# The mLSTM decay rows of a hybrid trunk are loaded through GpSimd's DMA queue instead of the sync engine's

## The chip, the cores and the metric

The kernel runs on one core of one Trainium2 chip. Its time is that of one execution on the device, in microseconds (us). The engines are named as in the profile: PE is TensorE's matmuls and PEld its weight loads, DVE is VectorE, ACT is ScalarE, POOL is GpSimd and SP is SyncE. A "q" behind an engine's name means its sequencer: SPq is the queue from which SyncE starts DMAs.

## What is computed

The reference is a decoder trunk of two layers over a sequence of 1024 positions with a width of 1024, in float32. In each layer one normalized input goes through one projection, and three groups of heads read it: an RG-LRU, a differential attention and an mLSTM. Their outputs are joined by one output projection; a causal conv-gated MLP follows. The change lies in the mLSTM, which the reference writes as a recurrence over chunks of 64 positions, for each of 4 heads of 128 features:

```python
D = jnp.where(causal, b[..., :, None] - b[..., None, :] + li[..., None, :], -jnp.inf)
m_t = jnp.maximum(m_inter, jnp.max(D, axis=-1))
w_intra = jnp.einsum('bhtd,bhsd->bhts', qc, kc) * jnp.exp(D - m_t[..., None])
inter = jnp.exp(m_inter - m_t)
num = inter[..., None] * jnp.einsum('bhtd,bhde->bhte', qc, C) + jnp.einsum('bhts,bhse->bhte', w_intra, vc)
den = inter * jnp.einsum('bhtd,bhd->bht', qc, n) + jnp.sum(w_intra, axis=-1)
h = num / jnp.maximum(jnp.abs(den), jnp.exp(-m_t))[..., None]
```

Every weight between a query t and a key s is the score q.k times the exponential of a decay. The kernel keeps that shape, with chunks of 512 positions instead of 64.

## The kernel before

`hybrid_trunk` runs, for each of the two layers, `mixer` (the heads and the output projection) and `ffn`. Nearly all matmuls keep float32 accuracy by splitting each operand into a high and a low part (`split`, lines 128 to 130: the high part is written by ScalarE, line 129, the low part by VectorE, line 130) and by three matmuls (`mm3`, lines 137 to 139).

The mixer is a list of steps, given by hand for each layer (`ORDER`, line 32). Steps "z" project the mLSTM's inputs, "A" are the attention, "R" the RG-LRU, "M" the mLSTM heads, "y" and "w" the output projection. A step only says in which order the program is written. The instructions of each engine are put in order when the program is built, by priority and estimated time, so that in the trace the steps interleave; evacuations and splits of weights are written with a raised priority (`high_priority(PRI)`). On the chip every engine and every DMA queue then works through its own list in that order: an instruction that waits holds up what stands behind it on the same engine. Tiles come from pools: a tag has so many buffers (`bufs`), and a new tile waits until a buffer of its tag has been used for the last time.

`ml_rows` (line 661) computes the decays of a layer: 32 rows of 1024 numbers, one for each of 8 blocks of 128 keys and 4 heads. It stores them to the DRAM tensor `Rd` (line 709), from which the heads read them back.

`ml_head(l, h, hf)` (line 780) does one head for one half of the positions, eight times in each layer (steps M0 to M7, two for each head). The queries and keys are loaded from DRAM and split; then four blocks of 128 keys follow (`jj`, line 806), each with n = 512, 384, 256 or 128 queries:

- one row of `Rd` is loaded into a tile R of 128 partitions, the same row in each (line 812). Its buffers have the tag "mr" with three buffers, which it shares with E and with `kt` (line 757);
- GpSimd masks the diagonal block (`affine_select`, line 813), ScalarE takes the exponential (line 814);
- TensorE computes the scores `ms` (line 816); VectorE multiplies them with R (line 817);
- the product is split into W (lines 129 and 130), and three matmuls add it, times the values, to the output `pn` (line 821);
- GpSimd adds R to the running sum `ds` (line 823 or 825), from which TensorE later forms the denominators (`tail`, line 832).

In the second half (`hf` = 1) the state of the first half comes in ahead of the blocks: one more row of `Rd` is loaded into E in the same way (line 798); ScalarE takes its exponential, VectorE multiplies it with the queries, and GpSimd starts `ds` from it (line 805). At the end of the first half `ml_state_out` (line 751) forms that state.

All loads and stores of the heads are issued from SyncE (`nc.sync.dma_start`), and so are the weight loads (`wblock`, line 113). GpSimd issues two kinds: `rgacc`, where each RG-LRU block adds its squares to a sum in DRAM (line 461; the first block stores, the other three accumulate), and, in the MLP, weight pieces that are added onto others (line 1120). `rg_sum` (line 467) reads the finished `rgacc` back through SyncE; the store of the RG-LRU's output itself (`yd`, line 459) goes through SyncE too.

Of the kernel before, what the change touches and what calls it, by code (L numbers as in the profile page):

```python
# [17 lines left out]
P = 128  # L18
# [3 lines left out]
HALF = 512  # L22
# [32 lines left out]
class Trunk:  # L55
# [724 lines left out]
    def ml_head(self, l, h, hf):  # L780
        nc, d = self.nc, self.lay[l]
        if hf == 0:
            self.ml_state[h] = [self.o4("num"), self.sm("mpc", (P, 16)), None]
        num, pc, state = self.ml_state[h]
        kscale = 0.25 * P ** -0.5
        qst = self.st_half(self.mqd[h][:, hf * HALF : (hf + 1) * HALF])
        qh, ql = self.qkt("qh"), self.qkt("ql")
        self.split(qst, qh, ql)
        kst = self.st_half(self.mkd[h][:, hf * HALF : (hf + 1) * HALF])
        kh, kl = self.qkt("kh"), self.qkt("kl")  # L790
        self.split(kst, kh, kl)
        vh, vl = self.vv(self.mvd, h, hf)
        pn = self.aux()
        ds = self.tp.tile([P, HALF], F32, tag="ds", bufs=1, name=self.nm("ds"))
        if hf:
            ch, cl, nv = state
            E = self.tp.tile([P, HALF], F32, tag="mr", bufs=3, name=self.nm("E"))
            nc.sync.dma_start(E, self.Rd[16 + h : 17 + h, HALF:].broadcast_to([P, HALF]))
            nc.scalar.activation(E, E, AF.Exp, bias=self.mle[:, 16 + h : 17 + h])
            nc.vector.tensor_tensor(E, E, qst, ALU.mult)  # L800
            W = self.p4("W", F32R)
            wh, wl = W[:, :HALF], W[:, HALF:]
            self.split(E, wh, wl)
            self.mm3(pn, [((ch, cl), (wh, wl))], stop=False)
            nc.gpsimd.tensor_scalar(ds, E, nv, None, ALU.mult)
        for jj in range(4):
            j = 4 * hf + jj
            n = HALF - jj * P
            js = slice(jj * P, jj * P + P)
            o = slice(jj * P, HALF)  # L810
            R = self.tp.tile([P, HALF], F32, tag="mr", bufs=3, name=self.nm("R"))
            nc.sync.dma_start(R[:, :n], self.Rd[4 * j + h : 4 * j + h + 1, j * P : (hf + 1) * HALF].broadcast_to([P, n]))
            nc.gpsimd.affine_select(R[:, :P], R[:, :P], [[1, P]], ALU.is_ge, -1e30, base=0, channel_multiplier=-1)
            nc.scalar.activation(R[:, :n], R[:, :n], AF.Exp, bias=self.mla[:, j, h : h + 1])
            sc = self.sc.tile([P, S], F32, tag="sc", name=self.nm("ms"))
            self.mm3(sc[:, :n], [((kh[:, js], kl[:, js]), (qh[:, o], ql[:, o]))])
            nc.vector.scalar_tensor_tensor(R[:, :n], sc[:, :n], kscale, R[:, :n], ALU.mult, ALU.mult)
            W = self.p4("W", F32R)
            wh, wl = W[:, :n], W[:, HALF : HALF + n]
            self.split(R[:, :n], wh, wl)  # L820
            self.mm3(pn[:, o], [((vh[:, js], vl[:, js]), (wh, wl))], start=j == 0, stop=jj == 3)
            if j == 0:
                nc.gpsimd.tensor_scalar(ds, R[:, :n], 1.0, 0.0, ALU.mult, ALU.add)
            else:
                nc.gpsimd.tensor_tensor(ds[:, o], ds[:, o], R[:, :n], ALU.add)
        if hf == 0:
            self.ml_state[h][2] = self.ml_state_out(h, kst, (vh, vl))
        nc.scalar.copy(num[:, hf * HALF : (hf + 1) * HALF], pn)
        def tail():
            pd = self.aux()  # L830
            for i in range(4):
                nc.tensor.matmul(pd[:, i : i + 1], ds[:, i * P : (i + 1) * P], self.ones_1, start=True, stop=True)
            nc.scalar.activation(pc[:, 8 + 4 * hf : 12 + 4 * hf], pd[:, 0:4], AF.Abs)
            if hf == 0:
                return
            sq = self.o4("sq")
            nc.scalar.activation(sq, num, AF.Square)
            pq = self.aux()
            self.compact(pq, sq, self.ones_h)
            f, v, r = self.sm("mf", (P, 8)), self.sm("nv", (P, 8)), self.sm("nr", (P, 8))  # L840
            nc.vector.tensor_tensor(f, pc[:, 8:16], self.mem[:, :, h], ALU.max)
            nc.vector.reciprocal(f, f)
            nc.vector.tensor_tensor(v, pq[:, 0:8], f, ALU.mult)
            nc.vector.tensor_tensor(v, v, f, ALU.mult)
            nc.vector.tensor_scalar(v, v, EPS, None, ALU.add)
            self.rsqrt(r, v)
            nc.vector.tensor_tensor(r, r, f, ALU.mult)
            th = self.p4("th")
            nc.sync.dma_start(th, self.mod[h])
            nc.vector.scalar_tensor_tensor(num, th, 1.0, num, ALU.add, ALU.mult)  # L850
            for j in range(2):
                t = slice(j * HALF, (j + 1) * HALF)
                nc.vector.scalar_tensor_tensor(num[:, t], num[:, t], d["mn2"][:, h : h + 1],
                                               self.bcast_half(r, j, self.ps), ALU.mult, ALU.mult)
            self.yd[8 + h] = self.dr("yd")
            nc.sync.dma_start(self.yd[8 + h], num)

        if h == 3 and hf:
            tail()
        else:  # L860
            self.tails.append(("M", tail))
# [479 lines left out]
```

## Time and profile before

| | |
|---|---|
| three runs | 2951.89, 2963.69 and 2966.23 us; median 2963.69 us |
| the profiled execution | 2952.44 us; its span 2950.7 us |
| mean granted clock of TensorE | 0.991 of full speed |
| busy share of the span | PE 97%, PEld 79%, DVE 70%, ACT 46%, POOL 8% |
| DMA | 353.58 MB, 120 GB/s on average |
| chain that ended last | PE 79%, DVE 8%, DMA 6%, ACT 3%, issue 3%, POOL 1% |

The profile is one execution, and its durations belong to it. The busy share of TensorE comes from matmuls that overlap, so 97% doesn't mean that it works at its peak; what counts is where it stands idle, for whom, and at which clock it then runs (1.00 in the column PEclk is full speed, 2.4 GHz; 0.50 is 1.2 GHz). A wait is put down to the work that ended it. The chain is followed from the last instruction back, at each step to what released it. "L812" is line 812 of the kernel; a line inside a helper, such as 129 or 137, stands for all that call it.

### The profile page before, as it was taken

Reading aid. Unit: us, or ns where it says so; the run is one execution under the profiler, and the core shown is the slowest. Engines: PE = TensorE matmul, PEld = TensorE weight load, DVE = VectorE, ACT = ScalarE, POOL = GpSimd, SP = SyncE. Lnnn points to the kernel's source line nnn. Section 1 sums busy time; section 2 is a strip of 40 time slices with the busy share of each in tenths; the row PEclk is TensorE's granted clock in tenths of the full one; section 3 lists DMA queues with packets and bytes.
Section 4 is the critical chain, followed back from the end, with each engine's and each line's share of the span. In section 5 each row is a group of like instructions: output and inputs, shape, how many; then the busy total and the mean of one; then the engine's idle time right before and its main releaser. Section 6 shows DMA issues by size and latency. Waiting matters only on the chain.

```text
span 2950.7 us, 36646 instructions
## 1 busy us (share of the span) xinstructions
PE 2863.7 (97%) x13262; PEld 2322.1 (79%) x13262; DVE 2055.0 (70%) x3369; ACT 1343.7 (46%) x2154; POOL 248.4 (8%) x312
## 2 busy tenths in 40 slices
PE   8999999989999999999999999998999999999998
PEld 6877777777788888788777877787877888887887
DVE  5775778776798888743484388787758888887334
ACT  4424656643554444421342256566426544444224
POOL 1000001111100000000000000202111000000000
PEclk9999999999999999999999999999999999999999
DMA  4332223463344454532423222325533544446223
GB/s 151 99 110 77 90 90 96 141 206 121 118 119 127 126 129 122 190 128 75 143 87 98 100 76 93 106 87 173 170 113 115 132 129 125 116 113 230 89 74 111
DMA packets 177029, 353.58 MB, mean 120 GB/s; under 512 B 20656, under 2 KB 47792, under 8 KB 176848
## 3 DMA queue, kind: packets, MB, share of 16 engines
q1 hardware_dynamic: 162144, 323.19, 34.1%
q0 software_dynamic: 13824, 27.27, 5.6%
q8 instruction: 104, 1.70, 0.2%
q10 hardware_dynamic: 880, 0.79, 0.1%
q14 instruction: 77, 0.63, 0.1%
HBM read 264.66 MB, written 86.51 MB: 119 GB/s over the span
## 4 chain that ended last, share of the span: by engine, by line
PE 79%; DVE 8%; DMA 6%; ACT 3%; issue 3%; POOL 1%; SPq 0%; DVEq 0%; POOLq 0%; ACTq 0%
PE z L138 23%; PE z L139 23%; PE z L137 23%; DMA R<-Rd 2%; DMA fst<-fa 1%; PE pbc L217 1%; PE aux L223 1%; DVE wlo L130 1%; PE sc L616 1%; PE aux L137 1%; PE aux L138 1%; PE sc L617 1%; PE aux L632 1%; PE aux L139 1%; DMA rgacc<-rg 1%
## 5 line engine op out<-in xcount | busy, mean ns | idle before, releaser
L129 ACT CAST whi<-wraw 128x512 fp32r<-128x512 f32 (+1 forms) x416 | 254.0, 612 | 689.5 <-PE z L138 516.4
L130 DVE TENSOR_TENSOR wlo<-wraw,whi 128x512 fp32r<-128x512 f32 (+1 forms) x416 | 284.7, 685 | 149.8 <-ACT whi L129 147.7
L138 PE MATMUL z<-hl,whi 128*128 128x512 f32 x896 | 360.5, 402 | 4.7 <-DVE hl L242 4.7
L137 PE MATMUL z<-hh,whi 128*128 128x512 f32 x896 | 361.3, 403 | 0.8 <-DVE mpad L416 0.8
L139 PE MATMUL z<-hh,wlo 128*128 128x512 f32 x896 | 360.4, 402 | 0.0
L137 PE MATMUL z<-ah,whi 128*128 128x512 f32 x704 | 272.8, 393 | 6.0 <-ACT ah L129 6.0
L137 PE MATMUL z<-xh,whi 128*128 128x512 f32 x704 | 274.6, 391 | 3.4 <-ACT cv L1151 3.4
L138 PE MATMUL z<-xh,whi 128*128 128x512 f32 x704 | 274.9, 390 | 1.9 <-DVE xh L130 1.9
L138 PE MATMUL z<-ah,whi 128*128 128x512 f32 x704 | 274.8, 392 | 0.6 <-DVE ah L130 0.4
L139 PE MATMUL z<-ah,wlo 128*128 128x512 f32 x704 | 274.6, 391 | 0.0
L139 PE MATMUL z<-xh,wlo 128*128 128x512 f32 x704 | 273.7, 389 | 0.0
L1128 DVE SCALAR_TENSOR_TENSOR fc<-cv,fpar,fc 128x1024 f32<-128x1024 f32 x176 | 221.7, 1279 | 5.9 <-ACT fc L1125 0.6
L129 ACT CAST whi<-fraw 128x512 fp32r<-128x512 f32 x180 | 111.5, 619 | 249.8 <-PE z L138 245.4
L137 PE MATMUL z<-xu,whi 128*128 128x512 f32 x528 | 209.3, 396 | 0.6 <-ACT cv L1151 0.6
L138 PE MATMUL z<-xu,whi 128*128 128x512 f32 x528 | 208.9, 396 | 0.0
L139 PE MATMUL z<-xu,wlo 128*128 128x512 f32 x528 | 208.8, 396 | 0.0
L138 PEld LDWEIGHTS z<-hl,whi 128*128 128x128 f32 x896 | 171.7, 192 | 40.6 <-DVE hl L242 9.0
L137 PEld LDWEIGHTS z<-hh,whi 128*128 128x128 f32 x896 | 171.8, 192 | 32.2 <-DVE mpad L416 0.9
L139 PEld LDWEIGHTS z<-hh,wlo 128*128 128x128 f32 x896 | 171.7, 192 | 31.4
L137 PEld LDWEIGHTS z<-ah,whi 128*128 128x128 f32 x704 | 131.9, 188 | 38.1 <-ACT ah L129 9.1
L137 PEld LDWEIGHTS z<-xh,whi 128*128 128x128 f32 x704 | 132.2, 188 | 32.0 <-ACT cv L1151 3.7
L1151 DVE TENSOR_TENSOR cv<-z,cv 128x512 f32<-128x512 f32 x132 | 90.9, 688 | 95.1 <-PE z L139 95.0
(374 smaller groups left out, 6026.3 us busy)
## 6 DMA issues: line engine op xcount, KB each, us to landing
wraw<-in_w_up_dram SPq DMA_DIRECT2D x128, 256.0 KB, 3.7
wraw<-in_w_in_dram SPq DMA_DIRECT2D x112, 256.0 KB, 2.8
wraw<-in_w_down_dram SPq DMA_DIRECT2D x112, 256.0 KB, 2.7
fraw<-in_w_up_dram SPq DMA_DIRECT2D x92, 256.0 KB, 2.9
fraw<-in_w_up_dram POOLq DMA_DIRECT2D x88, 256.0 KB, 5.0
fa<-fc SPq DMA_DIRECT2D x44, 512.0 KB, 3.9
fa<-fa SPq DMA_DIRECT2D x28, 512.0 KB, 5.3
wraw<-in_w_out_dram SPq DMA_DIRECT2D x48, 256.0 KB, 2.7
```

Of the source, the lines that this page charges most:

```text
L129: self.nc.scalar.copy(hi, src)
L130: self.nc.vector.tensor_tensor(lo, src, hi.bitcast(F32), ALU.subtract)
L137: nc.tensor.matmul(out, ah, bh, start=start and i == 0, stop=False, **kw)
L138: nc.tensor.matmul(out, ah, bl, start=False, stop=False, **kw)
L139: nc.tensor.matmul(out, al, bh, start=False, stop=stop and i == last, **kw)
L217: nc.tensor.matmul(pb[:, i * P : (i + 1) * P], r[:, c : c + 1].broadcast_to([P, P]), self.ident, start=True, stop=True)
L223: self.nc.tensor.matmul(pc[:, i : i + 1], sq[:, i * P : (i + 1) * P], ones, start=True, stop=True)
L616: nc.tensor.matmul(dst, qq[c][:, qs], k[:, :kn], start=True, stop=False)
L617: nc.tensor.matmul(dst, ql[c][:, qs], k[:, :kn], start=False, stop=kb < g)
L632: nc.tensor.transpose(pa[:, k * P : (k + 1) * P], pp[0][:, (4 * kb + k) * P : (4 * kb + k + 1) * P], self.ident)
L1128: nc.vector.scalar_tensor_tensor(o, u[:, j : j + S], cw[:, j, col : col + 1], o, ALU.mult, ALU.add)
L1151: fn(*x)
```

## The change

The two loads from `Rd` in `ml_head` are issued from GpSimd's queue instead of SyncE's. Their sources, destinations, sizes and buffers stay as they are: 4 loads of R in each of 8 steps in each of two layers, 64 in all, and 8 of E.

```diff
-            nc.sync.dma_start(E, self.Rd[16 + h : 17 + h, HALF:].broadcast_to([P, HALF]))
+            nc.gpsimd.dma_start(E, self.Rd[16 + h : 17 + h, HALF:].broadcast_to([P, HALF]))
...
-            nc.sync.dma_start(R[:, :n], self.Rd[4 * j + h : 4 * j + h + 1, j * P : (hf + 1) * HALF].broadcast_to([P, n]))
+            nc.gpsimd.dma_start(R[:, :n], self.Rd[4 * j + h : 4 * j + h + 1, j * P : (hf + 1) * HALF].broadcast_to([P, n]))
```

## Rows read from the trace of the kernel before

**Rows 1.** page, part 1: busy us (share of the span) xinstructions of each engine

```profile
PE 2863.7 (97%) x13262; PEld 2322.1 (79%) x13262; DVE 2055.0 (70%) x3369; ACT 1343.7 (46%) x2154; POOL 248.4 (8%) x312
```

**Rows 2.** mixers' stretches: us, each engine's busy us, PEclk, DMA share, GB/s

```profile
150.00:700.00 550.00, 526.31 (x2643) 426.94 (x2644) 400.89 (x731) 286.94 (x502) 60.52 (x83) 0.98 0.37 115
...
1560.00:2180.00 620.00, 596.75 (x2962) 482.44 (x2961) 427.85 (x795) 306.80 (x534) 67.62 (x87) 0.98 0.35 112
```

**Rows 3.** TensorE's waits, whole span: us in total, times, longest us

```profile
PE aux L137 <- ACT W L129: 8.9, 4, 6.0
PE aux L832 <- POOL ds L825: 7.8, 9, 2.3
...
PE aux L138 <- DVE W L130: 7.1, 8, 1.5
```

**Rows 4.** chain that ended last, heads: by line; pieces (start, us, what)

```profile
by line: PE z L139 9.1%; PE z L138 9.0%; PE z L137 8.7%; DMA R<-Rd 7.1%; issue 4.7%; PE aux L223 4.0%; PE pbc L217 3.2%; PE aux L138 2.6%; PE aux L139 2.4%; PE aux L137 2.4%; DVE wlo L130 2.4%; POOL ds L825 2.3%; PE aux L632 2.2%; DVE W L13
...
436.08 3.81 DMA E<-Rd
...
683.82 6.34 DMA R<-Rd
...
697.25 3.14 DMA R<-Rd
...
by line: DMA R<-Rd 10.8%; PE z L139 9.4%; PE z L138 9.2%; PE z L137 8.9%; issue 6.9%; PE aux L223 3.8%; POOL ds L825 2.7%; PE pbc L217 2.7%; DMA st<-vd 2.0%; DVE W L130 2.0%; PE aux L137 1.9%; DVE wlo L130 1.9%; PE aux L138 1.9%; DVE R L817
...
1855.55 2.77 DMA R<-Rd
...
2054.13 5.09 DMA R<-Rd
```

**Rows 5.** line 812's DMAs of R: ns min/median/max on the queue; us to landing

```profile
L812 SPq DMA_DIRECT2D R<-Rd x64: 319/320/895, 154.4 to 2150.3; - x64
...
DMA to landing us min/median/max: 2.8/4.2/6.9
```

**Rows 6.** the sync queue's own waits, whole span: us in total, times, longest us

```profile
SPq L113 <- DVE wlo L130: 724.2, 219, 16.3
...
SPq L812 <- DVE W L130: 70.1, 32, 8.0
...
SPq L467 <- DMA rgacc<-rg: 9.4, 2, 6.5
```

**Rows 7.** two lines on GpSimd: its DMAs, its sums: ns min/median/max

```profile
L1120 POOL DMA_DIRECT2D fraw<-in_w_up_dram x88: 842/863/1188, 735.6 to 2638.3; - x88
...
L825 POOL TENSOR_TENSOR ds<-ds,R x56: 455/1020/2600, 417.8 to 2155.6; 128x384 f32<-128x384 f32 x16, 128x256 f32<-128x256 f32 x16, 128x128 f32<-128x128 f32 x16, 128x512 f32<-128x512 f32 x8
```

**Rows 8.** 512 KB transfers to landing: line 461 (GpSimd); yd among the issues

```profile
DMA to landing us min/median/max: 4.2/5.5/7.3
...
yd<-rg SPq DMA_DIRECT2D x8, 512.0 KB, 2.6
```

**Rows 9.** timeline near 2050 us: start us, us, engine, line [idle before <-releaser]

```profile
2053.71 0.32 SPq L467 DMA_DIRECT2D rgs<-rgacc  x1
2054.13 0.37 SPq L812 DMA_DIRECT2D R<-Rd  x1
...
2048.18 0.90 POOL L461 DMA_DIRECT2D rgacc<-rg  x1 [2.47 <-ACT rg L460]
...
2049.28 1.49 DVE L130 TENSOR_TENSOR W<-R,W 128x512 fp32r<-128x512 f32 x3
...
2061.45 0.48 PE L137 MATMUL aux<-W,vh 128*128 128x128 f32 x1 [6.00 <-ACT W L129]
```

**Rows 10.** stretches of 5 us after the episode, columns as in rows 2

```profile
2055.00:2060.00 5.00, 0.45 (x2) 0.02 (x1) 0.00 (x0) 0.33 (x2) 0.29 (x1) 0.82 0.69 228
2060.00:2065.00 5.00, 3.55 (x14) 3.34 (x14) 4.05 (x6) 3.22 (x6) 0.46 (x1) 0.50 0.78 290
...
2075.00:2080.00 5.00, 5.00 (x16) 3.92 (x15) 2.08 (x5) 2.33 (x4) 1.11 (x2) 0.63 0.21 84
```

## The prediction, made before the change was run

> **What bounds the kernel now.** I read the page first: TensorE is busy 97% of the span and GpSimd 8%, so GpSimd has room for more work and TensorE has little idle time to give back [rows 1]. The table of stretches says where that idle time can lie. The two mixers, which hold all the loads that the change moves, leave TensorE idle 23.7 us of 550 and 23.3 us of 620, at a mean granted clock of 0.98 [rows 2]. In the list of TensorE's waits, the three kinds that belong to the mLSTM heads come to 8.9 + 7.8 + 7.1 = 23.8 us: for the weights W made from the decay rows (on ScalarE and on VectorE), and for GpSimd's sum ds [rows 3]. These loads can therefore win some 20 us and what hangs on the clock, and no more; what they can lose has no such limit.
>
> Are the loads on the path? The chain that ended last says yes: R<-Rd is 7.1% of it in the first mixer's heads and 10.8% in the second's. Its pieces there are 14 of the 72 moved loads: 13 of R and one of E. Six of them took 2.77 to 3.14 us; they ran with little beside them. Eight took 3.81 to 6.34 us [rows 4]. One of the eight, issued at 2054.13, is an episode of its own (below).
>
> **What leaves the sync queue.** The 64 loads of R occupy that queue 0.32 us each, and I take the same for the 8 of E: 72 x 0.32 = 23 us [rows 5]. The queue also stands 70.1 us, in 32 waits, before loads of R whose buffer isn't free, with everything behind them held up [rows 6]. What would profit is chiefly the weight loads of line 113. They wait 724.2 us for their own buffers, so they are issued as soon as a buffer comes free [rows 6], and no wait of TensorE for weights stands among the three large ones [rows 3]. I take 0, with the weight buffers as the cover; if that cover were thin, the gain would be part of the 23 us.
>
> **What GpSimd takes on.** A DMA on GpSimd is an instruction of the engine: the 88 that exist took 0.86 us in the median [rows 7]. So 72 x 0.86 = 62 us are added to 248 us of busy time. Nearly all of it falls into GpSimd's idle time; on the path it can only delay ds, for which TensorE waited 9 times (7.8 us). One DMA ahead of each of these sums costs 9 x 0.86 = 7.7 us, none costs 0. I take 4 us, one in two, because the last sum of a head has only the next head's loads near it.
>
> **A load from the other queue lands later.** No load of this kind went through GpSimd before, so I bound the difference. Upper: the rgacc transfer from GpSimd lands 5.5 us after issue in the median, the store yd of the same size from SyncE 2.6 us, which is +2.9 (six of the eight rgacc transfers accumulate, so this is high). Lower: the fastest rgacc transfer, 4.2 us, less 2.6 is +1.6 [rows 8]. A plain broadcast load is nearest to the plain end, so I take +1.6. A loss of nothing is not excluded for loads that now queue: R's median to landing is 4.2 us against a minimum of 2.8 [rows 5], and on a queue of their own they no longer stand behind a 256 KB load issued just before. The six quick loads of the chain then cost 6 x 1.6 = 9.6 us (at most 6 x 2.9 = 17.4). The seven slow ones, without the episode, now take 3.81, 5.33, 3.99, 6.34, 5.55, 5.80 and 5.68 us, 5.2 on average; at 2.8 + 1.6 = 4.4 to 2.8 + 2.9 = 5.7 us each changes by -0.8 to +0.5, together -5.7 to +3.5. I take -1, near the middle.
>
> **The episode.** At 2048.18 GpSimd issues the last accumulation into rgacc. SyncE then waits 6.5 us for it in order to read it back, and issues that read at 2053.71; only then, at 2054.13, the load of R that stood behind it in the queue. VectorE had split the earlier W tiles from 2049.28, so this load's buffer was free near 2050. TensorE meanwhile stands still for 6.00 us until 2061.45 [rows 9]. The granted clock then stays at 0.50, the lower of its two levels (1.2 for 2.4 GHz): 0.82 in the stretch from 2055, 0.50 in the three from 2060, 0.63 in the one from 2075 [rows 10]. That is 1.8 + 15 + 3.7 = 20.5 us at the lower level, of which 3.3 fall into the standstill; the other 17.2 us did 8.6 us' worth of work. So the episode costs 6.0 + 8.6 = 14.6 us. On GpSimd's queue the load waits for its buffer alone. Issued at 2050.0 to 2050.8 and landing 4.4 to 5.5 us later it is there at 2054.4 to 2056.3 instead of 2059.2: 2.9 to 4.8 us of the stall go, and I expect the long spell at the lower clock to shrink by 7 to 8.6 us. That is -9.9 to -13.4 us; I take -12. What is late next is the same load, by the 1.2 to 3.1 us that are left.
>
> **The sum.** 0 + 4 + 9.6 - 1 - 12 = +0.6 us; with the bounds, from 0 + 0 + 9.6 - 5.7 - 13.4 = -9.5 to 7.7 + 17.4 + 3.5 - 9.9 = +18.7. The profiled execution took 2952.44 us, its span 2950.7 us. The three runs shown are 2951.89, 2963.69 (the median) and 2966.23, so the profiled one lies 11.25 us under the median and beside the fastest. The sum is made against the profiled execution; for the forecast I set it on the mean of all four, 2958.6, which gives 2959, and I say **2960 us**. Differences within 0.5% (14.8 us) can't be told from no change here.
>
> **The rivals.**
> Slower, by GpSimd's queue being one line. A load that waits there for its buffer, as 32 loads of R now do on the sync queue for up to 8.0 us, keeps the mask and the sums behind it waiting, and each load lands late by the upper price. For it: these waits pass over whole [rows 6]. Against it: what stands behind mostly needs the same buffers. The price is 17.4 for the quick loads, 7 x (2.9 - 1.4) = 10.5 for the others (1.4 being their share of queueing that goes, 4.2 - 2.8), 7.7 for ds, less 9.9: +25.7 us, some 2984. It decides once a moved load of the chain takes over 5.9 us to land: their mean is now 4.15, and 13 x (5.9 - 4.15) + 4 - 12 is 14.8.
> Faster: the episode goes whole (-14.6) and the loads' own queue repays the later landing, so that R lands in about 4.2 us as before. Some shorter stalls for W go with it, say 4 of their 16 us. That is about -18, some 2941. For it: in the episode it is the queue's order, not the memory, that holds the load.
> Slower, by VectorE holding GpSimd off. GpSimd's instructions do stretch: the sums of line 825 took 1.02 us in the median and 2.60 at most, 1.6 more [rows 7]. If each of the 13 loads' issues stretches so, the sum is 0.6 + 20.8, some 2980. Against it, the 88 DMAs that GpSimd issues beside a VectorE busy for 70% of the span took at most 1.19 us. The Trainium skill (SBUF — State Buffer, section "Who interferes with whom") states such a rule: a DMA whose descriptors GpSimd writes is blocked while VectorE holds the shared port, and one that takes about 620 ns alone took about 3100 ns. By that rule each load would cost 2.5 us more, an estimate of +33 on the 13; the trace doesn't bear it out for the VectorE operations that run here.
> That the queue moves but little else does is my forecast itself. One thing I can't price: the order of instructions on each engine is chosen when the program is built, by priorities and estimated times, and a load on another queue can reorder it, for better or worse.
>
> **How the numbers follow.** No change 0.40, the faster rival 0.22, slower by the line 0.32, slower by VectorE 0.06. The forecast's own range is -9.5 to +18.7 on the lowest level and on the mean, 2943 to 2977. The range for 8 in 10 reaches into the slower case to take in its 2984, and leaves out the faster case's lower half: 2943 to 2988. Faster 0.22, same 0.40, slower 0.38.
>
> **What would show it.** Right: GpSimd busy near 310 us with 72 more DMAs at about 0.86 us; R landing in 4.4 to 5.5 us; the 6.00 us stall near 2061 gone or under 3.1 us, and no spell of 20 us at the lower clock there; waits for ds up by some 4 us. Wrong towards slower: new TensorE stalls for W in the heads, at more than ten places, or GpSimd's DMAs well over 1.2 us. Wrong towards faster: R landing in 4.2 us or less and the waits for W down. If the order on TensorE differs widely, differences outside the heads say that none of these steps decided.

## The result and the profile after

| | before | after |
|---|---|---|
| median | 2961.45 us (7 runs, 2951.89 to 2966.23) | 2979.02 us (7 runs, 2971.92 to 2986.09) |
| profiled execution; its span | 2952.44 us; 2950.7 us | 2981.69 us; 2979.8 us |
| mean granted clock, profiled execution | 0.991 | 0.982 |
| mean granted clock over many runs | 0.9873 (31 runs, beside the first experiments) | 0.9837 (the 7 runs) |

The change made the kernel slower: the ratio is 1.0058, with an interval of 1.0045 to 1.007. Run again later, beside other kernels, it gave 1.0063 (1.0044 to 1.0082). That is 17.6 us in the medians, where the forecast was no change.

The page, busy time of each engine and the chain that ended last, against [rows 1] and [rows 4]:

```profile
PE 2887.4 (97%) x13262; PEld 2341.0 (79%) x13262; DVE 2051.9 (69%) x3369; ACT 1342.3 (45%) x2154; POOL 282.1 (9%) x384
...
PE 77%; DVE 8%; issue 5%; DMA 4%; ACT 3%; POOL 2%; SPq 0%; DVEq 0%; POOLq 0%; ACTq 0%
```

Read the first line in two steps. GpSimd has 72 more instructions and 34 us more work. TensorE has the same 13,262 matmuls, but they took 23.7 us longer. The rest of the span, in which it stood idle, grew only from 87.0 to 92.4 us. So in these two executions most of the 29 us is not waiting: it is the same work at a lower clock. Busy time by mean clock gives the same product, 2863.7 x 0.991 = 2838 and 2887.4 x 0.982 = 2835 us. Stretches at 1.2 GHz add up to 54.9 us in 9 spells before and 109.9 us in 19 spells after.

The profiled execution of before lies 9 us under the median of its runs, so the means of many runs are fairer: the span is 2958.4 us at 0.9873 and 2976.3 us at 0.9837. Span times mean clock, run by run, is 2920.9 and 2927.8 us on the average: an estimate of the span at full clock. By it about 7 us of the 17.9 are added waits, and 11 come with the clock. In the later round it is 4 and 11.

The list of TensorE's waits after (engine, line, for whom; us in total, times, longest us), against [rows 3]:

```profile
PE aux L832 <- POOL ds L825: 13.5, 12, 2.2
...
PE aux L138 <- DVE W L130: 5.5, 7, 1.8
...
PE aux L137 <- ACT W L129: 3.0, 3, 1.4
```

The wait of 6.00 us for W has gone, and the waits for ds grew from 7.8 to 13.5 us. The moved loads themselves, in the view of DMAs by line (ns min/median/max on the queue, first and last start; below, us from issue to landing), against [rows 5]:

```profile
L812 POOL DMA_DIRECT2D R<-Rd x64: 534/556/902, 156.4 to 2178.5; - x64
...
DMA to landing us min/median/max: 3.1/3.8/7.5
...
L798 POOL DMA_DIRECT2D E<-Rd x8: 547/559/567, 427.9 to 2161.3; - x8
...
DMA to landing us min/median/max: 3.6/4.0/5.4
```

They land in 3.8 us in the median (before: 4.2), and one issue takes 0.56 us. In the chain of the heads only four pieces R<-Rd are left, of 3.14 to 3.46 us, where there were thirteen [rows 4]. By these rows alone the change looks like a success. The table of stretches shows what speaks against it (columns as in [rows 2]):

```profile
150.00:700.00 550.00, 523.30 (x2561) 424.39 (x2561) 389.43 (x712) 278.48 (x486) 70.74 (x109) 0.96 0.37 112
1560.00:2180.00 620.00, 596.68 (x2926) 480.00 (x2925) 422.99 (x782) 305.59 (x535) 80.12 (x120) 0.97 0.36 111
```

The clock fell from 0.98 to 0.96 and 0.97 in the two mixers (elsewhere by 0.01 at most), and fewer instructions fit into the same stretch (2561 matmul records for 2643). Measured at the same landmarks of the program, the profiled execution after is 1.5 us behind by 477 us and 21 us behind at the end of layer 0's heads (736 us). It is 23 us behind when layer 1's mixer begins and 29 us at the end. These landmarks come from one execution each and don't place the loss by themselves: the kernel with only layer 1's loads moved (below) runs layer 0 in the order and on the queues of before, and its profiled execution was 13 us behind before's when layer 1's mixer began.

**Another order.** The two programs differ in more than the queue. TensorE's built list has 1691 lines of difference. In the order in which the two profiles show the instructions, VectorE's 3369 differ in 306 lines and ScalarE's 2154 in 196 (an instruction that stands elsewhere counts twice). A load on another queue has another place and another estimated time in the list.

### The profile page after: what moved, and what is told of

Same layout as the page of the kernel before. It is cut to its first block, busy times and chain, and to the rows that moved or that the text cites. A ratio compares the mean times of both kernels' runs of the same rounds, so it can differ in the third digit from the quotient of the medians.

```text
span 2979.8 us, 36580 instructions
## 1 busy us (share of the span) xinstructions
PE 2887.4 (97%) x13262; PEld 2341.0 (79%) x13262; DVE 2051.9 (69%) x3369; ACT 1342.3 (45%) x2154; POOL 282.1 (9%) x384
## 4 chain that ended last, share of the span: by engine, by line
PE 77%; DVE 8%; issue 5%; DMA 4%; ACT 3%; POOL 2%; SPq 0%; DVEq 0%; POOLq 0%; ACTq 0%
PE z L137 23%; PE z L139 23%; PE z L138 23%; PE sc L616 1%; PE aux L223 1%; PE pbc L217 1%; DVE wlo L130 1%; DMA fst<-fa 1%; PE sc L617 1%; PE aux L632 1%; PE aux L138 1%; POOL ds L825 1%; PE aux L137 1%; PE aux L139 1%; DMA rgacc<-rg 1%
## 5 line engine op out<-in xcount | busy, mean ns | idle before, releaser
L137 PEld LDWEIGHTS z<-ah,whi 128*128 128x128 f32 x704 | 132.7, 189 | 38.0 <-ACT ah L129 8.9
L138 PEld LDWEIGHTS z<-ah,whi 128*128 128x128 f32 x704 | 132.8, 189 | 30.2 <-DVE ah L130 1.3
```

Of the source, the lines that this page charges most:

```text
L137: nc.tensor.matmul(out, ah, bh, start=start and i == 0, stop=False, **kw)
L138: nc.tensor.matmul(out, ah, bl, start=False, stop=False, **kw)
```

## The experiments

Two theories stood at the start. **Queue theory:** a load on GpSimd's queue costs by itself, by its issue, its landing, and what it holds up in GpSimd's line. **Order theory:** the loads cost nothing, but the new order of all engines' instructions does, with more small stalls and more falls of the clock. All ratios below are to the kernel before, run on the same chip in the same rounds (2959.6 to 2963.9 us in the median there). The rows rest on 7 to 10 executions each, those of the change again and of layer 0 alone on 4. The ratios of the plain medians can differ from the ones shown, by 0.0013 at most.

| kernel | loads on GpSimd | TensorE's order | ratio (interval) |
|---|---|---|---|
| change | 72 | changed | 1.0058 (1.0045 to 1.007) |
| change again | 72 | changed | 1.0063 (1.0044 to 1.0082) |
| only E | 8 | its own (1431 lines from before) | 1.0036 (1.002 to 1.0052) |
| only late blocks | 32 | its own (281 lines) | 1.0047 (1.0031 to 1.0064) |
| ScalarE's queue | 0 | its own (1757 lines) | 1.0026 (1.001 to 1.0041) |
| rgacc read back by GpSimd | 0 | its own (33 lines) | 1.0011 (0.9999 to 1.0023) |
| order of before kept | 44 | of before | 1.0002 (0.9989 to 1.0015) |
| one load | 1 | its own (129 lines) | 0.9978 (0.9964 to 0.9991) |
| one load again | 1 | its own (129 lines) | 0.9986 (0.997 to 1.0002) |
| E first in the source | 0 | its own (841 lines) | 1.0015 (1.0001 to 1.0029) |
| changed order kept, 38 back | 34 | changed | 1.0022 (1.001 to 1.0035) |
| the three loads back | 69 | changed | 1.0049 (1.0032 to 1.0067) |
| the other 35 back | 37 | changed | 1.004 (1.0025 to 1.0054) |
| layer 0 alone | 36 | half changed | 1.0058 (1.0041 to 1.0076) |
| layer 1 alone | 36 | half changed | 1.0008 (0.9992 to 1.0024) |

**Parts of the change.** Only E's eight loads, then only R's loads of the last two blocks:

```diff
-            nc.sync.dma_start(E, self.Rd[16 + h : 17 + h, HALF:].broadcast_to([P, HALF]))
+            nc.gpsimd.dma_start(E, self.Rd[16 + h : 17 + h, HALF:].broadcast_to([P, HALF]))
```

> Only the 8 loads of E go to GpSimd's queue; the 64 of R stay on SyncE's. Queue theory (a load on GpSimd's queue is itself what costs): 8 of 72 loads, so 8/72 of the 17.6 us between the medians, about 2 us over the kernel before, with the sums ds waited for hardly more than its 7.8 us. Order theory (another queue makes the build put every engine's instructions in another order, and that order lets TensorE's clock fall more often): the list of TensorE differs from that of before in 1431 lines, nearly as many as the change's 1691, so the time can come out 5 to 20 us off with hardly any load moved, and the difference is in the granted clock, not in the waits.

```diff
-            nc.sync.dma_start(R[:, :n], self.Rd[4 * j + h : 4 * j + h + 1, j * P : (hf + 1) * HALF].broadcast_to([P, n]))
+            (nc.gpsimd if jj > 1 else nc.sync).dma_start(R[:, :n], self.Rd[4 * j + h : 4 * j + h + 1, j * P : (hf + 1) * HALF].broadcast_to([P, n]))
```

> The 32 loads of R of the third and fourth key block (those that mostly wait for a buffer) go to GpSimd's queue, all others stay on SyncE's. TensorE's list differs from that of before in 281 lines only. Queue theory: at least 32/72 of 17.6 us, about 8 us over the kernel before, up to all 17 if the waits for buffers are what costs; waits for ds go up towards 13 us. Order theory: within 5 us of the kernel before, granted clock 0.99.

Eight of 72 loads cost 1.0036, over half of the whole loss, while TensorE waited less for ds than before (5.2 us for 7.8). Eight loads at such a price are not a price per load. The 32 late ones cost 1.0047, with ds waits of 12.2 us, though their order differs least of the three. That one is for the queue theory, or for an order that is bad in few places; the two can't be told apart here.

**The same loads on a third queue.** All 72 issued from ScalarE:

```diff
-            nc.sync.dma_start(E, self.Rd[16 + h : 17 + h, HALF:].broadcast_to([P, HALF]))
+            nc.scalar.dma_start(E, self.Rd[16 + h : 17 + h, HALF:].broadcast_to([P, HALF]))
...
-            nc.sync.dma_start(R[:, :n], self.Rd[4 * j + h : 4 * j + h + 1, j * P : (hf + 1) * HALF].broadcast_to([P, n]))
+            nc.scalar.dma_start(R[:, :n], self.Rd[4 * j + h : 4 * j + h + 1, j * P : (hf + 1) * HALF].broadcast_to([P, n]))
```

> All 72 loads are issued from ScalarE's queue, none from GpSimd's. TensorE's list differs from that of before in 1757 lines. Queue theory: GpSimd is as free as before, so waits for ds stay near 8 us and the time is that of before within 5 us, or slower only as far as new waits for ScalarE show. Order theory: clock and time change as for any other order, 5 to 20 us either way, without such waits.

Half of the loss, 1.0026, without one load on GpSimd. At 645 us TensorE waits in this kernel for VectorE's `mnv`, ahead of the second half of the sixteen broadcasts (timeline):

```profile
645.16 2.04 PE L217 MATMUL pbc<-identr,rgr 128*128 128x128 f32 x8 [4.70 <-DVE mnv L777]
```

The changed kernel has the same split at this place, and before does not have it. First the timeline of before, then of after:

```profile
633.08 2.05 PE L217 MATMUL pbc<-identr,rgr 128*128 128x128 f32 x16 [1.23 <-ACT num L828]
```

```profile
643.93 2.07 PE L217 MATMUL pbc<-identr,rgr 128*128 128x128 f32 x8 [0.86 <-ACT num L828]
...
647.03 1.19 PE L217 MATMUL pbc<-identr,rgr 128*128 128x128 f32 x4 [1.03 <-DVE mnv L777]
```

This is what another order looks like: a row of 16 short matmuls with one wait ahead of it has become two rows of 8 with a wait ahead of each. The stretches of 5 us around it, first before, then after (the column behind the five busy times is the granted clock):

```profile
630.00:635.00 5.00, 3.77 (x34) 3.69 (x34) 2.21 (x5) 2.98 (x6) 0.00 (x0) 1.00 0.98 370
635.00:640.00 5.00, 5.00 (x29) 4.39 (x28) 4.25 (x5) 3.31 (x6) 2.77 (x2) 1.00 0.85 236
```

```profile
640.00:645.00 5.00, 4.08 (x29) 3.74 (x29) 1.57 (x3) 1.44 (x3) 1.09 (x2) 0.82 1.04 330
645.00:650.00 5.00, 3.97 (x18) 3.61 (x18) 2.00 (x5) 3.58 (x7) 0.58 (x2) 0.50 0.59 172
650.00:655.00 5.00, 5.00 (x16) 4.32 (x17) 2.22 (x2) 1.11 (x2) 2.54 (x1) 0.50 0.17 58
655.00:660.00 5.00, 5.00 (x20) 4.03 (x19) 2.95 (x4) 3.23 (x5) 0.00 (x0) 0.82 0.19 53
```

After, the clock is at its lower level for 13.65 us from 643.2, so the spell begins in the wait ahead of the first row, and the split can only have lengthened it. The one row of 16 can be met by a fall too: of the nine profiles that have it here four show none within 20 us and five one of 3.4 to 10.2 us. The seven profiles with two rows of 8 all show one, of 10.2 or 13.65 us. On the average that is 12.2 us at the lower level for 3.0, an estimate of 4.6 us of time at this place.

**The order kept.** Which queue a load is on can be set for each load. 44 loads were found (43 of R, one of E) that go to GpSimd's queue while TensorE's and VectorE's instructions stand exactly as before:

```diff
-            nc.sync.dma_start(R[:, :n], self.Rd[4 * j + h : 4 * j + h + 1, j * P : (hf + 1) * HALF].broadcast_to([P, n]))
+            (nc.gpsimd if (l, h, hf, jj) in GP else nc.sync).dma_start(R[:, :n], self.Rd[4 * j + h : 4 * j + h + 1, j * P : (hf + 1) * HALF].broadcast_to([P, n]))
```

`GP` by layer, head and half: the blocks jj, and E for the load of E (jj = -1 in the set; line 798 is written in the same way):

```
000: 0 1 2 3; 001: 1 2 3; 010: 2 3; 011: 0 1 2 3
020: 0 1 2 3; 021: 1 2; 030: 1 2 3; 031: 1
100: 0 1 2 3; 101: 2 3; 110: 1 2 3; 111: 0 1 2 3
120: 0; 121: E 1 2; 130: 2; 131: 1 2 3
```

> 43 loads of R and one of E go to GpSimd's queue, chosen so that TensorE's and VectorE's instructions stand in exactly the order of the kernel before (ScalarE's differ in 57 lines, GpSimd's in 193). Queue theory: the sums ds come late behind the loads and masks on GpSimd, so TensorE's waits for ds go from 7.8 to 11 us or more, span times granted clock rises by 4 us or more over before (2921, mean of 31 runs), and the time by 11 us (44/72 of the gap of about 18) or more. Order theory: with the order unchanged the clock stays at before's 0.987 and the time within 4 us of before.

1.0002: 44 loads cost nothing that the interval shows; it ends at 1.0015, 4.4 us. They are not quite free. The waits for ds and, on ScalarE, for W come to 9.8 + 13.7 us in this profile (before: 7.8 + 8.9), and span times mean clock is 3.6 us above that of before in the same rounds, while the mean clock is no lower (0.9866 for 0.9862).

**The order changed, no load moved:** E's load stands in the source ahead of the loads of queries and keys, all on SyncE:

```diff
+        if hf:
+            E = self.tp.tile([P, HALF], F32, tag="mr", bufs=3, name=self.nm("E"))
+            nc.sync.dma_start(E, self.Rd[16 + h : 17 + h, HALF:].broadcast_to([P, HALF]))
         qst = self.st_half(self.mqd[h][:, hf * HALF : (hf + 1) * HALF])
...
-            E = self.tp.tile([P, HALF], F32, tag="mr", bufs=3, name=self.nm("E"))
-            nc.sync.dma_start(E, self.Rd[16 + h : 17 + h, HALF:].broadcast_to([P, HALF]))
```

> No load changes its queue: all stay on SyncE's. Only the place of E in the program is changed (its load stands ahead of those of the queries and keys), which gives TensorE another order, 841 lines of its list, without line numbers. Order theory: time and clock move by 5 us or more either way although GpSimd's queue is as before and the waits for ds stay near 8 us. Queue theory: within 4 us of the kernel before.

1.0015, with no queue changed. It is a small loss, and by its interval hardly more than none.

**The counterpart.** 38 of the 72 loads go back to SyncE, chosen so that TensorE's and VectorE's order is that of the changed kernel (the same two lines; `GP` now holds the other 34):

```
001: E 0 2; 010: 1; 011: E 2; 020: 2
021: E 0 1 3; 030: 0 2; 031: E 0 1 2; 101: E 0 1 2 3
110: 1; 111: E; 120: 0 2 3; 121: 1 3
130: 0 2; 131: E 0 3
```

> 38 of the 72 loads (37 of R, one of E) go back to SyncE's queue, chosen so that TensorE's and VectorE's instructions stand in exactly the order of the changed kernel; 34 loads stay on GpSimd's. It is the counterpart of the kernel with 44 loads on GpSimd and the order of before. Order theory: the time of the changed kernel, ratio 1.004 to 1.007 (2973 to 2982 us). Queue theory: with 34 of 72 loads 34/72 of the +17.6 us, +8.3 us, ratio 1.003 or less, and near that kernel's 1.0002.

1.0022: neither theory's number. The changed order with 34 loads costs some 7 us; how much of that is the order alone isn't separated here. The 38 other loads cost 12 us more by the ratios (1.0063 less 1.0022) and 7.6 us by the medians of the same rounds (2975.72 and 2968.15), with four executions on one side. So the queue does cost in the changed order. Of these 38 loads 31 are among the 44 that cost so little in the old one.

**Where.** Layer 0's loads alone, layer 1's alone (the load of E in the same way), and the change once more beside them:

```diff
-            nc.sync.dma_start(R[:, :n], self.Rd[4 * j + h : 4 * j + h + 1, j * P : (hf + 1) * HALF].broadcast_to([P, n]))
+            (nc.gpsimd if l == 0 else nc.sync).dma_start(R[:, :n], self.Rd[4 * j + h : 4 * j + h + 1, j * P : (hf + 1) * HALF].broadcast_to([P, n]))
```

> Only layer 0's 36 loads are on GpSimd's queue, layer 1's stay on SyncE's. In the two profiled executions 23 of the 29 us come before layer 1's mixers and 6 in them. Order theory: the loss follows the places where the order came out badly, so it is unequal: 23/29 of the +17.6 us, +14 us, ratio about 1.0047, with TensorE's idle time and the time at the lower clock growing in layer 0's heads from 556 to 736 us. Queue theory: half of the loads, half of the loss, +9 us, 1.003.

> Only layer 1's 36 loads are on GpSimd's queue; the load of R at 2054 us is one of them. Order theory: 6/29 of the +17.6 us, +3.6 us, ratio about 1.0012, layer 0 to the us as before. Queue theory: half of the loads, half of the loss, +9 us, 1.003.

> The changed kernel itself once more, on the same chip and in the same rounds as the three beside it, so that they can be set against it: both theories 1.0045 to 1.007.

1.0058 and 1.0008: nearly the whole loss is in layer 0, and the two together give the whole. Layer 1's moved loads win and lose about the same.

**What the queue holds up.** The three profiles of kernels with all of layer 0's loads on GpSimd (the change, the change again, layer 0 alone) have the same two stalls there, near 563 and 673 us, and the kernel with 38 loads back does not have them. The first, near 563 us, in the timelines of after and of the kernel with 38 back (start, us, engine, line, in brackets idle before and releaser):

```profile
555.01 0.53 POOL L812 DMA_DIRECT2D R<-Rd  x1 [2.43 <-DVE W L130]
...
558.12 1.27 DVE L420 SCALAR_TENSOR_TENSOR rg<-mpad,par,rg 128x1024 f32<-128x1024 f32 x1
558.23 2.12 POOL L813 TENSOR_SCALAR_AFFINE_SELECT R<-R 128x128 f32<-128x128 f32 x1
...
559.31 0.88 DVE L130 TENSOR_TENSOR W<-R,W 128x384 fp32r<-128x384 f32 x2
...
560.38 0.40 ACT L814 ACTIVATE R<-R,mla 128x128 f32<-128x128 f32 x1 [1.65 <-POOL R L813]
...
563.13 0.33 PE L137 MATMUL aux<-W,vh 128*128 128x128 f32 x1 [1.41 <-ACT W L129]
```

```profile
558.93 0.33 SPq L812 DMA_DIRECT2D R<-Rd  x1
...
562.50 0.28 POOL L813 TENSOR_SCALAR_AFFINE_SELECT R<-R 128x128 f32<-128x128 f32 x1
562.51 1.35 DVE L420 SCALAR_TENSOR_TENSOR rg<-mpad,par,rg 128x1024 f32<-128x1024 f32 x1
```

With the load on SyncE the mask starts 0.01 us ahead of VectorE's operation and takes 0.28 us. With the load on GpSimd it starts 0.11 us behind it and takes 2.12 us: it ends 0.16 us after the second of the two splits of line 130 that follow on VectorE. The other three masks of over 0.9 us in this profile, and the nine in before's, ended 0.13 to 0.16 us after the VectorE operation that ran when they began. Set beside the kernel with 38 back by VectorE's operation, the exponential starts 1.75 us late and W 1.1 us; TensorE stands 1.41 us for W, and the clock is at its lower level for 6.8 us from 564.65. The second kind is in the heads of layer 1, near 2118 us, again after and then with 38 back:

```profile
2112.26 0.68 DVE L130 TENSOR_TENSOR W<-E,W 128x512 fp32r<-128x512 f32 x1
...
2114.81 0.59 POOL L812 DMA_DIRECT2D R<-Rd  x1 [17.20 <-DVE x L877]
...
2118.29 0.29 POOL L813 TENSOR_SCALAR_AFFINE_SELECT R<-R 128x128 f32<-128x128 f32 x1 [2.88 <-DMA R<-Rd]
2118.55 2.33 POOL L825 TENSOR_TENSOR ds<-ds,R 128x512 f32<-128x512 f32 x2
...
2119.86 0.38 PE L832 MATMUL aux<-ones,ds 128*128 128x1 f32 x2 [1.94 <-POOL ds L825]
```

```profile
2106.86 0.68 DVE L130 TENSOR_TENSOR W<-E,W 128x512 fp32r<-128x512 f32 x1
...
2107.61 0.32 SPq L812 DMA_DIRECT2D R<-Rd  x1
...
2110.59 0.29 POOL L813 TENSOR_SCALAR_AFFINE_SELECT R<-R 128x128 f32<-128x128 f32 x1 [16.58 <-DVE mu L420]
...
2111.26 1.30 POOL L825 TENSOR_TENSOR ds<-ds,R 128x512 f32<-128x512 f32 x1 [0.38 <-DVE R L817]
```

The buffer comes free when the split of E ends. SyncE issues 0.07 us later; GpSimd issues 1.87 us later here, and 0.54 us later after most splits of W. The mask then waits 2.88 us for the load, and behind the mask in GpSimd's line stands the sum ds, whose own input was ready before the mask began. TensorE waits 1.94 us for that sum. The stall hangs on the late issue: the same load is on GpSimd's queue in the kernel with layer 1's loads alone too, was issued 0.58 us after its buffer was free, and TensorE waited 0.70 us there. The next experiment takes these two loads and one like the second (near 673 us) back, and the one after it takes the other 35 (there the set lists the 37 that stay on GpSimd):

```diff
-            nc.gpsimd.dma_start(R[:, :n], self.Rd[4 * j + h : 4 * j + h + 1, j * P : (hf + 1) * HALF].broadcast_to([P, n]))
+            (nc.sync if (l, h, hf, jj) in BACK else nc.gpsimd).dma_start(R[:, :n], self.Rd[4 * j + h : 4 * j + h + 1, j * P : (hf + 1) * HALF].broadcast_to([P, n]))
```

with `BACK = {(0, 1, 1, 3), (0, 2, 1, 2), (1, 2, 1, 2)}` in the first.

> The changed kernel with 3 of its 72 loads of R back on SyncE's queue: layer 0 head 1, second half, jj 3; layer 0 head 2, second half, jj 2; layer 1 head 2, second half, jj 2. TensorE's, VectorE's and ScalarE's instructions stand exactly as in the changed kernel. In its two profiles each of these loads lands late ahead of a mask on GpSimd, and TensorE then waits 1.4 us (for W, near 563 us), 1.3 us (for ds, near 673 us) and 1.9 us (for ds, near 2120 us), each wait followed by a fall of the clock of 3.4 to 6.8 us. Three-places theory (of the loss that the order leaves over, most is these three loads): waits down by 1.2, 0.9 and 1.3 us, three falls gone, together 3.4 + 6.8 = about -9 us against the changed kernel, ratio 1.002 to 1.003, as the kernel with 38 loads back. Spread theory (each of the 38 loads back is worth the same, 7.6/38 = 0.2 us): -0.6 us, ratio 1.0055 to 1.006.

> The complement: 35 loads go back to SyncE's queue, and those three stay on GpSimd's with the other 34; TensorE's and VectorE's order is that of the changed kernel. Three-places theory: as the changed kernel, 1.005 to 1.006. Spread theory: -7 us, ratio 1.0025.

1.0049 and 1.004. Both theories get a part: with 34 loads 1.0022, with the three more 1.004, with the 35 more 1.0049, with all 1.0063. By the ratios the three cost 0.0014 to 0.0018, some 4 to 5 us or 1.5 us each; the 35 cost 0.0023 to 0.0027, some 7 to 8 us or 0.2 us each. Each step is about as wide as its uncertainty (0.002 to 0.0026), and the kernels were run in two rounds, so this division is likely and not shown. By the medians over before, the three cost 2.9 us and the 35 cost 4.7. With the three back, two of the three waits went as expected. With the 35 back, the waits of layer 0 stayed (1.41 and 1.27 us), but the one in layer 1 shrank to 0.70 us though its load was still on GpSimd's queue (issued 0.57 us after its buffer was free). With the three back, the third wait, near 673 us, moved on to the next load, as the timeline of the kernel with the three back shows:

```profile
678.28 0.28 POOL L813 TENSOR_SCALAR_AFFINE_SELECT R<-R 128x128 f32<-128x128 f32 x1 [1.10 <-DMA R<-Rd]
678.54 0.45 POOL L825 TENSOR_TENSOR ds<-ds,R 128x128 f32<-128x128 f32 x1
...
679.04 0.38 PE L832 MATMUL aux<-ones,ds 128*128 128x1 f32 x2 [1.34 <-POOL ds L825]
```

All three loads are among the 44 that cost next to nothing in the order of before. There GpSimd's longest mask is 1.31 us.

**The episode by itself.** The prediction's largest gain was the load of R issued at 2054.13 [rows 9]. First its cause alone: `rgacc` is read back through GpSimd, the loads stay on SyncE.

```diff
-        self.nc.sync.dma_start(t, self.rgacc)
+        self.nc.gpsimd.dma_start(t, self.rgacc)
```

> The kernel before with one edit: the sum rgacc is read back through GpSimd's queue (2 loads) instead of SyncE's; all loads of R and E stay on SyncE's. TensorE's list differs in 33 lines. If the 6.00 us stall and the 20.5 us at the lower clock near 2058 us came from that read standing in SyncE's queue, both go: 14.6 us faster, about 2947. Rival: the stall only moves to the next late load, 0 to 5 us faster.

A miss: the stall stayed (6.30 us). The load of R then stood behind another load in SyncE's queue that waited for the same transfer (timeline):

```profile
2061.38 0.32 SPq L871 DMA_DIRECT2D x<-xd  x1
2061.62 0.57 POOL L467 DMA_DIRECT2D rgs<-rgacc  x1 [4.81 <-DMA rgacc<-rg]
2061.81 0.37 SPq L812 DMA_DIRECT2D R<-Rd  x1
```

Then this one load alone on GpSimd's queue, `GP = {(1, 2, 0, 3)}`, twice:

> One load alone goes to GpSimd's queue: R of the fourth key block of head 2, first half, second layer, the one that was issued at 2054.13 in the kernel before; TensorE's list differs in 129 lines, all behind that point. If the episode is worth what the prediction says, the 6.00 us stall and the 20 us at the lower clock go and the time falls by 10 to 14.6 us, to 2945 to 2950. Rival: the stall goes, but the clock falls all the same in the thin work around it (transposes, one-column matmuls), and the gain is the stall alone, 3 to 6 us; or another late step takes its place, and it is 0.

> The kernel with one load of R on GpSimd's queue (layer 1 head 2, first half, jj 3) once more, since it was the fastest of eight and the fastest of eight looks better than it is. If its 0.9978 was the load: 0.9965 to 0.999 again. If it was the choice of the best: within 0.9995 to 1.0005.

0.9978 and 0.9986: 2957.0 and 2956.7 us, faster than before in both, though the second interval just reaches 1. The timeline of the first, and its stretches of 5 us (columns as in [rows 10]):

```profile
2052.86 0.58 POOL L812 DMA_DIRECT2D R<-Rd  x1 [1.31 <-DVE W L130]
...
2059.68 0.33 PE L137 MATMUL aux<-W,vh 128*128 128x128 f32 x1 [1.65 <-ACT W L129]
```

```profile
2060.00:2065.00 5.00, 4.76 (x26) 3.99 (x24) 2.76 (x4) 0.15 (x1) 0.00 (x0) 0.74 0.90 283
2065.00:2070.00 5.00, 3.10 (x15) 3.10 (x15) 2.15 (x4) 2.94 (x5) 0.00 (x0) 0.50 0.90 353
2070.00:2075.00 5.00, 5.00 (x18) 4.42 (x18) 2.32 (x6) 0.68 (x2) 1.00 (x1) 0.50 0.60 205
2075.00:2080.00 5.00, 5.00 (x14) 3.86 (x14) 2.82 (x7) 3.33 (x4) 1.06 (x3) 0.56 0.65 211
```

The load is issued 3.3 us before the read back (2056.14) and no longer behind it, and the stall shrinks from 6.00 to 1.65 us. But the clock falls all the same, for 17.1 us. This is the only version that beat both kernels.

Moving this load isn't enough in every order. Among the 32 late blocks it was on GpSimd's queue too and was issued 3 us ahead of the read back, and the stall stayed (timeline of that kernel):

```profile
2062.80 0.56 POOL L812 DMA_DIRECT2D R<-Rd  x1 [1.63 <-DVE W L130]
...
2065.77 0.32 SPq L467 DMA_DIRECT2D rgs<-rgacc  x1
...
2066.74 0.37 SPq L798 DMA_DIRECT2D E<-Rd  x1
...
2067.99 0.29 DVE L817 SCALAR_TENSOR_TENSOR R<-ms,R 128x128 f32<-128x128 f32 x1 [1.72 <-ACT R L814]
...
2072.55 0.72 ACT L799 ACTIVATE E<-E,mle 128x512 f32<-128x512 f32 x1 [4.08 <-DMA E<-Rd]
2073.18 0.28 ACT L129 CAST W<-R 128x128 fp32r<-128x128 f32 x1
...
2073.51 0.47 PE L137 MATMUL aux<-W,vh 128*128 128x128 f32 x1 [6.16 <-ACT W L129]
```

R is ready for its split at 2068.28. But in this order the exponential of E stands ahead of the split in ScalarE's line, and E's load, on SyncE, was issued behind the read back. TensorE waits 6.16 us for the same W.

## Why the prediction was wrong

**Its failed step** is the one it put last: "One thing I can't price: the order of instructions on each engine". It then counted that at nothing and gave its chances to the queue alone. The runs put the order with 34 loads at 1.0022, some 7 us, and two other orders without one load on GpSimd at 1.0015 and 1.0026. And they show that what the queue costs depends on the order: 44 loads cost at most 4.4 us in one, 38 loads, 31 of them the same, cost some 8 to 12 us in the other (by the medians or by 1.0063 less 1.0022). A sum over the rows of before could not hold this, because it prices each load at a place that the changed program no longer has.

**SyncE's relief, taken as 0.** No run contradicts it; it wasn't measured alone.

**GpSimd's work, 62 us, of it 4 us on the path.** The busy time rose by 34 us, for an issue took 0.56 us and not 0.86, and the sums of line 825 became a little shorter (0.99 us in the median for 1.02). The waits for ds rose by 5.7 us in the one profile of after and by 7.7 in the other: the step was right, and its 0 to 7.7 held both, though the 4 us it took was low. What it missed is how a sum comes late: not by one issue ahead of it, but behind a mask that waits for its load.

**Later landing, +1.6 us for each quick load.** Mis-sized. From issue to landing the minimum is 3.1 us for 2.8, and the median 3.8 for 4.2: the transfer rgacc, stored from GpSimd, was a bad stand-in for a broadcast load. What a load on GpSimd loses comes before that, the 0.3 to 0.6 us from the free buffer to the issue in most cases, and behind it, in the line.

**The episode, -12 us.** Right about the stall in part: it went in the change and shrank to 1.65 us with the one load alone, but with the 32 late blocks it stayed at 6.16 us, because E's load had the place behind the read back. Wrong about the clock: of the 14.6 us the 6 were the stall and 8.6 the spell at 1.2 GHz, and that spell stays when the stall shrinks. One load alone gained 4 to 6.5 us. In the changed kernel, too, most of the spell is still there: its clock is at 0.50 for 13.65 us from 2087.

**The rivals.** "GpSimd's queue being one line" named the mechanism that the last timelines show, a mask that waits for its own load and keeps ds behind it. Its point of decision was wrong: it asked for landings above 5.9 us on the average of the chain's loads, and waits of 1 to 2 us at few places, with a fall of the clock that can follow each, came without them. "VectorE holding GpSimd off" was priced on the DMAs, and there it isn't seen: 534 to 902 ns for the 64 loads of R, beside a VectorE that is busy 69% of the span. The Trainium skill (SBUF — State Buffer, section "Who interferes with whom") has that rule for VectorE's two-port modes, and says that `tensor_tensor`, which has none, did not stall a DMA. The trace agrees: 2028 us of VectorE's 2231, durations added up, are tensor_tensor and scalar_tensor_tensor. Whether the rule holds for the two-port modes no run here shows. The same section also says that a VectorE instruction with two inputs in SBUF contends with a GpSimd instruction that reads SBUF, and that whichever issues first wins. With that the trace agrees, on the mask: 0.28 us when it starts 0.01 us ahead of VectorE's operation, 2.12 us when it starts 0.11 us behind. That it there lost to three operations in a row, and not to the first alone, isn't explained.

**Its own test** was half right. "If the order on TensorE differs widely" came true, but the differences that it then looked for outside the heads lie in the mixers: the clock fell there, and from 736 us to layer 1's mixer the lag grew by 2 us only. That 2979 us lies inside 2943 to 2988 is in part luck: the upper end was set by a rival whose late landings didn't come. And 0.5%, which it took for no change, could be told: the intervals over 7 to 10 executions are some 0.15% to either side.

**What stays open.** Of the 35 other loads' 5 to 8 us no place was singled out. Why the 32 late blocks alone cost 1.0047 with so little reordering isn't explained; their profiled execution, the fastest of theirs, shows the waits for ds and for W up (12.2 us and, on ScalarE, 12.4 us) and little of the clock. Why E's eight loads alone cost 1.0036 is as open. The place of the sixteen broadcasts carries 4.6 us of the order's own 7 by the estimate from sixteen profiles; its split was not tried by itself. Why GpSimd issued the load at 2114.81 1.87 us after the buffer was free is not known. Both profiles of the change show it, and in both the issue comes 0.03 us or less after the end of the VectorE operation that the row names (line 877), which has nothing to do with R; in the four other kernels that have this load on GpSimd's queue it took 0.56 to 0.58 us.

## What to carry to other kernels

Moving a transfer to another queue in a program whose order is chosen at build time moves other instructions too. Compare the built order of every engine first, and test the queue with the order held and the order with the queue held. Move the one load that a wait shows to be blocked (here 1 of 72) rather than all loads of its kind, and look whether another load takes its place behind what blocked it. Before a load goes to an engine that also works on its data, look at what stands behind the consumer in that engine's line: here a sum whose input was ready waited for a mask whose load was late.

## What the runs showed of the hardware

Small waits cost more than their length. The same 13,262 matmuls were busy for 2863.7 us at a mean clock of 0.991 and for 2887.4 us at 0.982. Waits of 1.3 to 2 us between short matmuls were often followed by 3.4 to 13.65 us at 1.2 GHz; when the stall ahead of one spell shrank from 6.00 to 1.65 us, the spell shrank only from 20.5 to 17.1. The executions of the kernel before, 19 to 31 in a round, spread over 13 to 20 us, and their span goes with their mean clock (correlation -0.74 to -0.83). A single profile can therefore mislead: before's lay 9 us under its median.

A broadcast load of one row to 128 partitions takes GpSimd 0.56 us to issue and lands in 3.1 us at best; from SyncE it takes 0.32 us and 2.8 us.

GpSimd's mask of 128x128 took 0.29 us in the median. When it began while a VectorE operation with two inputs ran, it could last until 0.15 us after that operation's end, 1.34 us at most before the change; once, near 563 us, it waited through three of them (2.12 us).
